# Memory attention: scores of two heads per matmul, transpositions four at a time in a two-bank tile

## The chip, the cores and the metric

The kernel runs on one core of one Trainium2 chip. The metric is the time of one execution on the device, in microseconds (us). Engines are named as in the profile: PE (TensorE, matrix products and transpositions), PEld (its loading of weights), DVE (VectorE), ACT (ScalarE), POOL (GpSimd) and SP (SyncE, which here only issues DMAs).

## The reference, cut to what matters

The reference is one decoder layer over 1024 tokens of width 1024, in float32: a mixer (spatial gating and differential attention), attention to a memory of 256 tokens, and a mixture of 32 experts. The change lies in the memory attention:

```python
q = (hq @ w_q).reshape(Bn, Sn, MEM_HEADS, MEM_HEAD_DIM) * (MEM_HEAD_DIM ** -0.5)
kv = (mem_n @ w_kv).reshape(Bn, Mn, 2, MEM_HEADS, MEM_HEAD_DIM)
k, v = kv[:, :, 0], kv[:, :, 1]
s = jnp.einsum('bqhd,bkhd->bhqk', q, k).astype(jnp.float32)
p = jax.nn.softmax(s, axis=-1)
o = jnp.einsum('bhqk,bkhd->bqhd', p.astype(v.dtype), v).reshape(Bn, Sn, MEM_WIDTH)
return o @ w_o
```

Sn is 1024 and there are 4 heads of 256 memory tokens.

## The kernel before, in words

The kernel multiplies the keys into the query weights, and the values into the output weights, ahead of time. For each head the product of w_q and the keys is a matrix of 1024 x 256 (`md`), written to DRAM by `mem_m` and read back as weights of 512 KB by the queue of SP. The scores of a tile of 128 tokens are then the normalized hidden state (`h2`, eight tiles of 128 rows) times `md`, and the probabilities of all heads times `vwd` give the result of the attention (`mem_out`). Every product of float32 is three matmuls of a rounded half and a remainder (`mm3`, lines 136 to 138); `split` makes the two halves, the rounded one by a cast on ACT (L141), the remainder by a subtraction on DVE (L142). Weights are split the same way (L280 on ACT, L281 on DVE).

The scores (`mem_scores`) go head by head. A PSUM bank of 128 x 512 holds two tiles of tokens of one head: twice 24 matmuls of 256 columns. There are 4 heads x 2 halves of 512 tokens x 2 banks, so 16 banks. After each bank DVE takes the negative maximum of each row (L971) and scales it by the row's norm (L972), ACT computes the two exponentials with their sums (L974), DVE inverts the sums (L977), and POOL multiplies the probabilities by them (L979). When a head's half is done, `mem_values` transposes the probabilities on PE: 8 transposes of 128 x 128 (L1000), the first four into one PSUM bank (`pt`), the others into a second, and each bank is split into an `om` tile (L141, L142).

[...]

The program is emitted by generators that a small planner (`Merge`) interleaves by costs and delays in its own time: a `yield 1.3, 0.0` says that work of 1.3 was emitted, and the second number holds the generator back. Which engines keep the emitted order is set by `manual_schedule`: in this stage before the change SP and POOL do, while the order of PE, DVE and ACT is set by the framework's own scheduler. A wait between engines is put in by the framework wherever a tile is written after it was read, or read after it was written.

Of the kernel before, what the change touches and what calls it, by code (L numbers as in the profile page):

```python
# [8 lines left out]
F32 = mybir.dt.float32  # L9
# [11 lines left out]
KT = 8  # L21
H = 512
# [87 lines left out]
def tile_layer(tc, a, out):  # L110
# [12 lines left out]
    def unit(name, shape, dt=F32):  # L123
        return up.tile(shape, dt, name=name, tag="u", bufs=NU)
# [4 lines left out]
    def ps1(name="ps"):  # L129
        return psum.tile([128, 512], F32, name=name, tag="ps", bufs=4)  # L130

    def ps2(name="pd"):
        return psum.tile([128, 1024], F32, name=name, tag="pd", bufs=2)

    def mm3(o, sh, sl, mh, ml, start, stop):
        mm(o, sh, mh, start=start, stop=False)  # L136
        mm(o, sh, ml, start=False, stop=False)  # L137
        mm(o, sl, mh, start=False, stop=stop)  # L138

    def split(hi, lo, src):  # L140
        nc.scalar.copy(hi, src)  # L141
        nc.vector.tensor_sub(lo, src, hi.bitcast(F32))  # L142
# [71 lines left out]
    def add_pair(w, i):  # L214
        for q in range(2):
            plan.append((w[2 * i + q], 4))

    w_in8, w_in4 = a["w_in8"], a["w_in4"]
    for item in (SEQ1 + " " + SEQ2).split():
# [15 lines left out]
        else:  # L235
            w = a["w_q_memT" if kind == "m" else "w_o_mem"]
            for k in (2 * i, 2 * i + 1):
                plan.append((w[k * 128:(k + 1) * 128, :], 1))
    for hd in range(4):
        add_pair(md, hd)  # L240
    for h in range(2):
        for f in range(8):
            add_cols(vwd, f)
# [41 lines left out]
    def take():  # L285

        j = ptr["use"]
        ptr["use"] += 1
        pump()
        k = plan[j][1]  # L290
        return [t.rearrange("p (k c) -> p k c", k=k) for t in parts.pop(j)]
# [88 lines left out]
    def mem_m(hd):  # L380

        kk = kks.pop(("m", hd))
        w = [take() for _ in range(2)]
        for g in range(2):
            mt = unit("mt", [128, 4, 256])
            for b in range(2):
                p = ps1("pp")
                for j in range(2):
                    ds_ = slice((4 * g + 2 * b + j) * 128, (4 * g + 2 * b + j + 1) * 128)
                    for d in range(2):  # L390
                        mm3(p[:, j * 256:(j + 1) * 256], w[d][0][:, 0, ds_], w[d][1][:, 0, ds_], kk[:, 0, d],
                            kk[:, 1, d], d == 0, d == 1)
                nc.scalar.copy(mt[:, 2 * b:2 * b + 2], p)
                yield 1.3, 0.0
            nc.gpsimd.dma_start(md[2 * hd + g], mt.rearrange("p k c -> p (k c)"))

    def mem_w(hd):

# [535 lines left out]
    r2c = cp.tile([128, 8], F32, name="r2c")  # L934

    def r2_cols(h):
        p = ps1()
        colsum_out(h, p)
        rsq(r2c[:, 4 * h:4 * h + 4], p[:, 0:8:2], D / 256.0, 1e-6 * 256.0, "r")
        yield 0.9, 3.0  # L940
        done.add(("r2", h))
# [2 lines left out]
    om, P, rdy = {}, {}, {}  # L944

    def mem_scores():
        for hd in range(4):
            w = [take() for _ in range(2)]
            for h in range(2):
                if 2 * hd + h - nval[0] >= 2:  # L950
                    yield 0.0, lambda: 2 * hd + h - nval[0] < 2
                pe = unit("pe", [128, 4, 256])
                mx = sm.tile([128, 16], F32, name="mx", bufs=2)
                for t2 in range(2):
                    p = ps1("pp")
                    for j in range(2):
                        t = 4 * h + 2 * t2 + j
                        ts = slice(t * 128, (t + 1) * 128)
                        for k in range(KT):
                            wh, wl = w[k // 4]  # L960
                            mm3(p[:, j * 256:(j + 1) * 256], h2[k][0][:, ts], h2[k][1][:, ts], wh[:, k % 4],
                                wl[:, k % 4], k == 0, k == KT - 1)
                            if k == 3:
                                yield 1.3, 0.0
                        if j == 0:
                            yield 1.3, 0.0
                    for x in until(("r2", h)):
                        yield x
                    p3 = p.rearrange("p (t k) -> p t k", t=2)
                    i = 2 * t2  # L970
                    red(mx[:, i:i + 2], p3, axis=AX.X, op=OP.max, negate=True)  # L971
                    tt(mx[:, i:i + 2], mx[:, i:i + 2], r2c[:, 4 * h + i:4 * h + i + 2], op=OP.mult)  # L972
                    for j in range(2):
                        nc.scalar.activation(pe[:, i + j], p3[:, j], AF.Exp, bias=mx[:, i + j:i + j + 1],  # L974
                                             scale=r2c[:, 4 * h + i + j:4 * h + i + j + 1],
                                             accum_out=mx[:, 4 + i + j:5 + i + j])
                    nc.vector.reciprocal(mx[:, 8 + i:10 + i], mx[:, 4 + i:6 + i])  # L977
                    for j in range(2):
                        nc.gpsimd.tensor_scalar(pe[:, i + j], pe[:, i + j], mx[:, 8 + i + j:9 + i + j], 0.0,  # L979
                                                op0=OP.mult, op1=OP.add)  # L980
                    if t2 == 0:
                        yield 1.3, 0.0
                P[hd, h] = pe
                rdy[hd, h] = merge.t + 6.0
                done.add(("P", hd, h))
                yield 1.3, 0.0

    nval = [0]

    def mem_values():  # L990
        for hd in range(4):
            for h in range(2):
                for x in until(("P", hd, h)):
                    yield x
                yield 0.0, max(0.0, rdy[hd, h] - merge.t)
                pe = P.pop((hd, h))
                for b in range(2):
                    p = ps1("pt")
                    for t in range(4):
                        nc.tensor.transpose(p[:, t * 128:(t + 1) * 128], pe[:, t, b * 128:(b + 1) * 128], ident)  # L1000
                    x = unit("om", [128, 2, H], F32R)
                    split(x[:, 0], x[:, 1], p)
                    om[2 * hd + b, h] = x
                    yield 0.45, 0.0
                nval[0] += 1
                if hd == 3:
                    yield 0.0, 2.0
                done.add(("om", hd, h))


    desc = cp.tile([128, 8], F32, name="desc")
# [212 lines left out]
    def mem_out(hf):  # L1224
# [67 lines left out]
        for f, k0, k1 in todo:  # L1292
            if k0 == 0:
                x2 = half("x2")
                nc.sync.dma_start(x2, x1d[f * 128:(f + 1) * 128, hs])
                if hf:
                    ahead["load"] += PF
                grp[f] = (take(), ps1("pp"), x2)
            (wh, wl), p, x2 = grp[f]
            for k in range(k0, k1):  # L1300
                if k == 6:
                    for x in until(("om", 3, hf)):
                        yield x
                if (f, k) == (7, 5):
                    for t in range(4):
                        mm(plg[:, 160 + 2 * t:162 + 2 * t], acc["x2", hf][0][:, t * 128:(t + 1) * 128], ones[:, 0:2],
                           start=False, stop=False)
                o = om[k, hf]
                mm3(p, wh[:, k], wl[:, k], o[:, 0], o[:, 1], k == 0, k == KT - 1)
                if k in (1, 3, 5):  # L1310
                    yield 1.28, 0.0
            if k1 == 8:
                fin(f, p, x2)
                yield 1.28, 0.0
# [5 lines left out]
    def mem_end(hf):  # L1320
        for x in until(("mo", hf)):
            yield x
        last, plg, store = fini[hf]
        if hf:
            man = tc.manual_schedule(engines=RM)
            man.__enter__()
        else:
            yield 0.0, 0.8
        last()
        if hf:  # L1330
            for i in range(NX):
                xg.append(unit("xg", [128, D]))
                nc.gpsimd.memset(xg[i], 0.0)
            ahead["load"] += PG
            pump()
        yield 2.0, 3.0
        for x in route(hf, plg, store):
            yield x
        if hf:
            man.__exit__(None, None, None)  # L1340
# [21 lines left out]
    def first_consts():  # L1362
# [10 lines left out]
        for x in attn_lam():  # L1373
# [14 lines left out]
    man = tc.manual_schedule(engines=ORDS[2])  # L1388
    man.__enter__()
    ahead["load"], ahead["split"] = QL, QS  # L1390
    merge.run(r2_cols(0), r2_cols(1), mem_values(), mem_scores(), mem_end(0), mem_end(1),
              seq(until(RC), now(route_consts), now(load_gfb), mem_out(0), mem_out(1)))
    man.__exit__(None, None, None)


# [379 lines left out]
```

## Time and profile before

| | |
|---|---|
| time, median of 3 runs | 1393.46 us (1392.2 to 1393.85) |
| time of the profiled execution | 1396.04 us |
| its span on the core | 1394.3 us |
| PE busy | 1322.7 us, 95% of the span |
| DVE, ACT, POOL busy | 1001.3, 836.7, 255.7 us |
| DMA | 322.39 MB, mean 231 GB/s |

The span is what the trace shows, from the first instruction to the last; the profiled execution's own time is 1.7 us longer and lies 2.6 us above the median of the runs. Busy times are sums over an engine's instructions, and those of PE are pipelined: a matmul begins before the one before it has ended, so the time that one costs on PE is read from start to start. The granted clock of PE (PEclk) is 1.00 at full speed and 0.5 at half.

### The profile page before, as it was taken

How to read it: one execution, taken by the hardware profiler on the slowest of the kernel's cores; microseconds unless marked ns; L12 is line 12 of the kernel's file. 1: busy time of each engine (PE TensorE's matmuls, PEld its weight loads, DVE VectorE, ACT ScalarE, POOL GpSimd, SP SyncE). 2: the span in 40 equal slices, each digit the busy share in tenths (PEclk: the TensorE clock that was granted, in tenths of full speed). 3: DMA queues.
4: the chain of work that ended last, by engine and by line, in shares of the span. 5: the costliest groups of instructions: out<-in, count | busy, mean ns of one | idle time of the engine just before them, and what ended most of it. 6: DMA issues, size and time to landing. Idle time of an engine off the chain costs nothing. (4 is left out here: it accounts for less than half of the span.)

```text
span 1394.3 us, 20530 instructions
## 1 busy us (share of the span) xinstructions
PE 1322.7 (95%) x7424; PEld 1146.8 (82%) x7424; DVE 1001.3 (72%) x1564; ACT 836.7 (60%) x1139; POOL 255.7 (18%) x284
## 2 busy tenths in 40 slices
PE   7999999999989999999998899999989999999981
PEld 6988998989888889998886687888778888888861
DVE  6776694767765543434365798999979999999984
ACT  6644553445455543333323587888868888888874
POOL 2521110411021321112112121111111111111110
PEclk9999999999999999999998799999999999999995
DMA  8720211320275664103799799999999699999986
GB/s 306 220 84 15 47 61 46 91 69 16 101 266 188 201 243 143 38 25 110 241 331 336 244 322 369 364 355 357 354 366 351 226 371 381 366 366 363 373 287 256
DMA packets 103226, 322.39 MB, mean 231 GB/s; under 512 B 15748, under 2 KB 23972, under 8 KB 103121
## 3 DMA queue, kind: packets, MB, share of 16 engines
q1 hardware_dynamic: 76896, 272.14, 53.4%
q0 software_dynamic: 17776, 40.51, 10.1%
q10 hardware_dynamic: 8448, 8.39, 1.8%
q8 instruction: 59, 0.97, 0.3%
q14 instruction: 47, 0.38, 0.1%
HBM read 287.10 MB, written 46.66 MB: 239 GB/s over the span
## 5 line engine op out<-in xcount | busy, mean ns | idle before, releaser
L281 DVE TENSOR_TENSOR wlo<-raw,whi 128x1024 fp32r<-128x1024 f32 (+1 forms) x469 | 559.6, 1231 | 75.3 <-ACT whi L280 62.6
L280 ACT CAST whi<-raw 128x1024 fp32r<-128x1024 f32 (+1 forms) x469 | 472.7, 1050 | 69.2 <-DVE wlo L281 11.9
L136 PE MATMUL pgu<-whi,xth 128*128 128x512 f32 x512 | 199.4, 398 | 4.3 <-ACT whi L280 3.2
L137 PE MATMUL pgu<-wlo,xth 128*128 128x512 f32 x512 | 201.2, 393 | 0.8 <-DVE wlo L281 0.8
L138 PE MATMUL pgu<-whi,xtl 128*128 128x512 f32 x512 | 201.0, 393 | 0.5 <-DVE xtl L142 0.5
L1464 POOL DMA_INDIRECT x2d<-y,idx x31 | 51.6, 1666 | 449.4 <-ACT y L1463 411.5
L136 PEld LDWEIGHTS pgu<-whi,xth 128*128 128x128 f32 x512 | 97.0, 190 | 26.0 <-ACT whi L280 5.2
L137 PEld LDWEIGHTS pgu<-wlo,xth 128*128 128x128 f32 x512 | 97.2, 190 | 22.3 <-DVE wlo L281 1.4
L138 PEld LDWEIGHTS pgu<-whi,xtl 128*128 128x128 f32 x512 | 97.0, 189 | 21.2 <-DVE xtl L142 1.2
L137 PE MATMUL py<-wlo,ht 128*128 128x512 f32 x256 | 103.7, 405 | 2.2 <-DVE wlo L281 2.2
L136 PE MATMUL py<-whi,ht 128*128 128x512 f32 x256 | 102.3, 399 | 1.5 <-ACT whi L280 0.8
L138 PE MATMUL py<-whi,ht 128*128 128x512 f32 x256 | 101.0, 394 | 0.0
L658 ACT ACTIVATE p<-p,stt 128x128 f32<-128x128 f32 (+7 forms) x64 | 49.6, 776 | 50.4 <-DVE stt L657 45.9
L136 PE MATMUL pp<-whi,hTh 128*128 128x256 f32 x256 | 74.6, 291 | 0.2 <-ACT whi L280 0.2
L137 PE MATMUL pp<-wlo,hTh 128*128 128x256 f32 x256 | 73.4, 287 | 1.3 <-DVE wlo L281 1.3
L136 PE MATMUL pp<-whi,h2h 128*128 128x256 f32 x256 | 73.1, 285 | 0.0
L138 PE MATMUL pp<-whi,hTl 128*128 128x256 f32 x256 | 73.1, 285 | 0.0
L137 PE MATMUL pp<-wlo,h2h 128*128 128x256 f32 x256 | 72.5, 283 | 0.0
L138 PE MATMUL pp<-whi,h2l 128*128 128x256 f32 x256 | 72.5, 283 | 0.0
L136 PE MATMUL pp<-hTh,whi 128*128 128x512 f32 x160 | 63.6, 397 | 0.4 <-ACT ot L710 0.4
L137 PE MATMUL pp<-hTl,whi 128*128 128x512 f32 x160 | 63.0, 394 | 0.0
L138 PE MATMUL pp<-hTh,wlo 128*128 128x512 f32 x160 | 62.8, 393 | 0.0
(365 smaller groups left out, 2942.4 us busy)
## 6 DMA issues: line engine op xcount, KB each, us to landing
raw<-in_w_gate SPq DMA_DIRECT2D x128, 512.0 KB
raw<-in_w_up SPq DMA_DIRECT2D x128, 512.0 KB
raw<-in_w_down SPq DMA_DIRECT2D x128, 512.0 KB
raw<-in_w_in SPq DMA_DIRECT2D x19, 512.0 KB
raw<-in_w_kv_mem SPq DMA_DIRECT2D x16, 512.0 KB
raw<-vwd SPq DMA_DIRECT2D x16, 512.0 KB
raw<-in_w_q_memT SPq DMA_DIRECT2D x8, 512.0 KB
raw<-in_w_out SPq DMA_DIRECT2D x8, 512.0 KB
```

What stands on the lines that cost most here:

```text
L136: mm(o, sh, mh, start=start, stop=False)
L137: mm(o, sh, ml, start=False, stop=False)
L138: mm(o, sl, mh, start=False, stop=stop)
L280: nc.scalar.copy(hi[:, c], raw[:, c])
L281: ahead.get("lo", nc.vector).tensor_tensor(lo[:, c], raw[:, c], hi[:, c].bitcast(F32), op=OP.subtract)
L658: nc.scalar.activation(pe[:, :nk], pe[:, :nk], AF.Exp, bias=stt[:, 2 + m:3 + m], scale=slopes[hd], accum_out=stt[:, 4 + m:5 + m])
L1464: nc.gpsimd.indirect_dma_start(out=x2d[:, :], out_offset=bass.IndirectOffsetOnAxis(ap=idx[:, e:e + 1], axis=0), in_=y, in_offset=None, bou ...
```

## The change

- `mem_scores` works on two heads at a time: a bank holds one tile of tokens of both heads, from 24 matmuls of 512 columns. There are still 16 banks, but 384 matmuls instead of 768. Four weight tiles are taken per pair of heads, where two were taken per head.
- `md` is laid out by pairs of heads; `mem_m` therefore writes each 512 KB product by two DMAs with pieces of 1 KB instead of one.
- The multiplication of the probabilities by the inverted sums moves from POOL to DVE (32 TENSOR_SCALARs of 128 x 256).
- `mem_values` takes a two-bank tile per head and half; four transposes go to its first bank, four to the second, and by the planner's numbers (`yield 0.45, 1.3`) six matmuls of the scores stand between the two sets.
- Up to the end of the scores PE keeps the emitted order (`mem_order`); `mem_out` waits for `om` of the third and the fourth head apart.

```diff
-    for hd in range(4):
-        add_pair(md, hd)
+    for q in range(8):
+        plan.append((md[q], 2))
...
-            nc.gpsimd.dma_start(md[2 * hd + g], mt.rearrange("p k c -> p (k c)"))
+            for q in range(2):
+                nc.gpsimd.dma_start(
+                    md[4 * (hd // 2) + 2 * g + q].rearrange("p (k h t) -> p k h t", k=2, h=2)[:, :, hd % 2],
+                    mt[:, 2 * q:2 * q + 2])
...
     def mem_scores():
-        for hd in range(4):
-            w = [take() for _ in range(2)]
+        for hp in range(2):
+            w = [take() for _ in range(4)]
             for h in range(2):
...
+                for t in range(4):
                     p = ps1("pp")
+                    ts = slice((4 * h + t) * 128, (4 * h + t + 1) * 128)
+                    for k in range(KT):
+                        wh, wl = w[k // 2]
+                        mm3(p, h2[k][0][:, ts], h2[k][1][:, ts], wh[:, k % 2], wl[:, k % 2], k == 0, k == KT - 1)
+                        if k in (1, 3, 5):
+                            yield 1.36, 0.0
...
-                        nc.gpsimd.tensor_scalar(pe[:, i + j], pe[:, i + j], mx[:, 8 + i + j:9 + i + j], 0.0,
-                                                op0=OP.mult, op1=OP.add)
+                        nc.vector.tensor_scalar(pe[j][:, t], pe[j][:, t], mx[:, 2, 2 * t + j:2 * t + j + 1], None,
+                                                op0=OP.mult)
...
     def mem_values():
...
-                for b in range(2):
-                    p = ps1("pt")
+            pd = ps2("pt")
+            for b in range(2):
+                p = pd[:, b * H:(b + 1) * H]
...
-                    yield 0.45, 0.0
+                yield 0.45, 1.3
...
+    mem_order = tc.manual_schedule(engines={ET.PE})
+    mem_order.__enter__()
...
-              seq(until(RC), now(route_consts), now(load_gfb), mem_out(0), mem_out(1)))
+              seq(until(RC), now(mem_order.__exit__, None, None, None), now(route_consts), now(load_gfb), mem_out(0), mem_out(1)))
```

How the instructions stand on PE around the first transposes, before the change. A row is the place in PE's order, the line, the operation, its output and inputs (`pt` the transposed probabilities, `pe` the probabilities, `pp` a bank of scores), and the engines whose semaphores it waits for:

```order
3175 L137 MATMUL pp_5542<-wlo_5301,h2h_5304 128x256
3176 L138 MATMUL pp_5542<-whi_5300,h2l_5305 128x256
3177 L1000 MATMUL pt_5598<-ident_71,pe_5426 128x128 [waits Pool_49] x4
3178 L1000 MATMUL pt_5606<-ident_71,pe_5426 128x128 [waits DVE_49,Activation_49]
3179 L1000 MATMUL pt_5606<-ident_71,pe_5426 128x128 x3
3180 L136 MATMUL pp_5614<-whi_5227,h2h_4433 128x256 [waits DVE_49,Activation_49]
3181 L137 MATMUL pp_5614<-wlo_5228,h2h_4433 128x256
3182 L138 MATMUL pp_5614<-whi_5227,h2l_4434 128x256
3183 L136 MATMUL pp_5614<-whi_5227,h2h_4582 128x256
```

The eight transposes of the first head's first half stand in a row, into two tiles (`pt_5598`, `pt_5606`), and the next bank of scores follows. After the change, the same place:

```order
3152 L138 MATMUL pp_5582<-whi_5390,h2l_5313 128x512
3153 L1004 MATMUL pt_5614<-ident_71,pe_5406 128x128 [waits DVE_49] x4
3154 L136 MATMUL pp_5622<-whi_5235,h2h_4437 128x512 [waits PE_49,Activation_49]
3155 L137 MATMUL pp_5622<-wlo_5236,h2h_4437 128x512
3156 L138 MATMUL pp_5622<-whi_5235,h2l_4438 128x512
3157 L136 MATMUL pp_5622<-whi_5235,h2h_4588 128x512
3158 L137 MATMUL pp_5622<-wlo_5236,h2h_4588 128x512
3159 L138 MATMUL pp_5622<-whi_5235,h2l_4589 128x512
3160 L1004 MATMUL pt_5614<-ident_71,pe_5406 128x128 [waits DVE_49]
3161 L1004 MATMUL pt_5614<-ident_71,pe_5406 128x128 x3
3162 L136 MATMUL pp_5622<-whi_5308,h2h_4740 128x512
```

The first four transposes stand alone, then six matmuls of the next bank, then the second four into the same tile, `pt_5614`, with a wait for DVE at the first of them. The lines are those of the changed kernel (L1004 there is L1000 before).

The order of DVE around the same place before the change (`mx` holds the maxima and sums, `om` the split of the transposes):

```order
739 L971 TENSOR_REDUCE mx_5541<-pp_5542 128x2 [waits PE_49]
740 L972 TENSOR_TENSOR mx_5541<-mx_5541,r2c_91 128x2 [waits DVE_49]
741 L977 RECIPROCAL mx_5541<-mx_5541 128x2 [waits Activation_49]
742 L142 TENSOR_TENSOR om_5603<-pt_5598,om_5603 128x512 [waits Activation_49]
743 L142 TENSOR_TENSOR om_5611<-pt_5606,om_5611 128x512 [waits Activation_49]
744 L281 TENSOR_TENSOR wlo_5673<-raw_5420,whi_5672 128x1024 [waits DMAHW2_49,Activation_49]
```

After the bank's maximum, scaling and inversion come the subtractions of the transposes (`om`). After the change, where L973, L974, L979 and L981 are the maximum, its scaling, the inversion and the scaling of the probabilities:

```order
755 L973 TENSOR_REDUCE mx_5581<-pp_5582 128x2 [waits PE_49]
756 L974 TENSOR_SCALAR mx_5581<-mx_5581,r2c_91 128x2 [waits DVE_49]
757 L979 RECIPROCAL mx_5581<-mx_5581 128x2 [waits Activation_49]
758 L981 TENSOR_SCALAR pe_5579<-pe_5579,mx_5581 128x256 [waits DVE_49]
759 L981 TENSOR_SCALAR pe_5580<-pe_5580,mx_5581 128x256
760 L142 TENSOR_TENSOR om_5619<-pt_5614,om_5619 128x512 [waits Activation_49]
761 L142 TENSOR_TENSOR om_5633<-pt_5614,om_5633 128x512 [waits Activation_49]
762 L142 TENSOR_TENSOR om_5647<-pt_5642,om_5647 128x512 [waits Activation_49]
```

The subtraction that empties the first half of `pt_5614` (`om_5619`) stands behind all DVE work of the bank of scores that has just ended, the two new TENSOR_SCALARs included; it is that subtraction which the second four transposes wait for.

## Rows read from the trace of the kernel before

**Rows 1.** Windows: us, then busy of PE, PEld, DVE, ACT, POOL, clock, DMA share, GB/s
```profile
540.00:560.00 20.00, 20.00 (x170) 20.00 (x170) 7.95 (x32) 3.84 (x10) 1.88 (x4) 1.00 0.19 70
700.00:750.00 50.00, 50.00 (x279) 42.34 (x277) 27.55 (x69) 15.55 (x23) 11.98 (x12) 1.00 0.92 326
750.00:777.00 27.00, 16.16 (x109) 14.98 (x109) 17.81 (x63) 6.00 (x10) 6.73 (x6) 0.59 0.83 281
```

**Rows 2.** Groups by line and form, 538 to 660 us: names, shapes, count | busy us, mean ns
```profile
L136 PE MATMUL pp<-whi,h2h 128*128 128x256 f32 x256 | 73.1, 285 | 0.0
...
L979 POOL TENSOR_SCALAR pe<-pe,mx 128x256 f32<-128x256 f32 x32 | 15.1, 484 | 88.5 <-DVE mx L977 88.5
```

**Rows 3.** Timeline of PE at a bank's end: start us, busy us, line, names
```profile
555.07 0.28 PE L136 MATMUL pp<-whi,h2h 128*128 128x256 f32 x1
...
558.55 0.28 PE L138 MATMUL pp<-whi,h2l 128*128 128x256 f32 x1
558.67 1.04 PE L1000 MATMUL pt<-ident,pe 128*128 128x128 f32 x8
559.46 0.36 PE L136 MATMUL pp<-whi,h2h 128*128 128x256 f32 x1
```

**Rows 4.** Timeline of PE in the projection ahead, 512 columns a matmul
```profile
535.79 0.39 PE L136 MATMUL pp<-mixh,whi 128*128 128x512 f32 x1
...
537.15 0.39 PE L136 MATMUL pp<-mixh,whi 128*128 128x512 f32 x1
```

**Rows 5.** Timeline of VectorE after that bank, 558 to 563 us
```profile
558.87 0.69 DVE L971 TENSOR_REDUCE mx<-pp 128x2 f32<-128x512 f32 x1 [3.38 <-PE pp L138]
559.60 0.16 DVE L972 TENSOR_TENSOR mx<-mx,r2c 128x2 f32<-128x2 f32 x1
561.09 0.17 DVE L977 RECIPROCAL mx<-mx 128x2 f32<-128x2 f32 x1 [1.33 <-ACT pe L974]
561.56 1.29 DVE L142 TENSOR_TENSOR om<-pt,om 128x512 fp32r<-128x512 f32 x2 [0.31 <-ACT om L141]
```

**Rows 6.** Timeline of ScalarE after that bank
```profile
559.85 0.57 ACT L974 ACTIVATE pe<-pp,mx,r2c 128x256 f32<-128x256 f32 x1 [4.56 <-DVE mx L972]
...
560.86 0.20 ACT L974 ACTIVATION_READ_ACCUMULATOR pe<-pp,mx,r2c 128x1 f32 x1
560.95 1.07 ACT L141 CAST om<-pt 128x512 fp32r<-128x512 f32 x2
```

**Rows 7.** Groups by form of VectorE, whole span: its TENSOR_SCALARs nearest in form
```profile
L837 DVE TENSOR_SCALAR v<-v,mv,rs 128x128 f32<-128x128 f32 x32 | 8.6, 342 | 0.1
...
L1053 DVE TENSOR_SCALAR ra<-ra,c_norm_ffn 128x36 f32<-128x36 f32 x8 | 1.3, 236 | 0.0
```

**Rows 8.** Windows around three idle stretches of PE in the expert stage
```profile
789.00:792.00 3.00, 1.51 (x10) 0.83 (x7) 1.90 (x3) 2.46 (x4) 0.99 (x1) 1.00 0.85 288
792.00:796.00 4.00, 3.87 (x10) 3.08 (x11) 2.44 (x3) 1.76 (x2) 0.00 (x0) 0.57 0.74 229
842.00:845.00 3.00, 1.40 (x6) 0.58 (x5) 1.30 (x2) 2.37 (x3) 0.00 (x0) 1.00 1.03 418
845.00:848.00 3.00, 3.00 (x15) 2.52 (x16) 3.00 (x4) 3.00 (x4) 0.00 (x0) 1.00 1.00 384
1020.00:1024.00 4.00, 1.19 (x5) 0.41 (x3) 1.21 (x1) 2.29 (x3) 0.00 (x0) 1.00 1.02 403
1024.00:1028.00 4.00, 3.93 (x10) 3.11 (x11) 3.58 (x4) 3.32 (x4) 0.00 (x0) 0.57 0.94 363
```

**Rows 9.** Windows of the expert stage, its start and its middle
```profile
770.00:780.00 10.00, 8.37 (x34) 7.54 (x35) 6.58 (x9) 2.75 (x4) 5.00 (x4) 0.56 0.54 151
1100.00:1200.00 100.00, 100.00 (x479) 83.33 (x478) 92.01 (x86) 81.52 (x91) 17.73 (x12) 1.00 1.01 373
```

**Rows 10.** DMA issues, the products of the keys: queue, count, KB, us to landing
```profile
md<-mt POOLq DMA_DIRECT2D x8, 512.0 KB, 6.3
```

**Rows 11.** Timeline of VectorE at the start of the scores
```profile
538.64 2.35 DVE L281 TENSOR_TENSOR wlo<-raw,whi 128x1024 fp32r<-128x1024 f32 x2
```

More of the change, by code (lines that the diff above doesn't have):

```diff
@@ L936, in r2_cols @@
     def r2_cols(h):
+        yield 0.0, (1.3, 5.0)[h]
         p = ps1()
@@ L946, in mem_scores @@
     def mem_scores():
-        for hd in range(4):
-            w = [take() for _ in range(2)]
+        for hp in range(2):
+            w = [take() for _ in range(4)]
             for h in range(2):
[L950 to L954, printed above, removed]
-                    p = ps1("pp")
[L956 to L966, printed above, removed]
+                if 4 * hp + 2 * h - nval[0] >= 3:
+                    yield 0.0, lambda: 4 * hp + 2 * h - nval[0] < 3
+                pe = [unit("pe", [128, 4, 256]) for _ in range(2)]
+                mx = sm.tile([128, 3, 8], F32, name="mx", bufs=2)
+                for t in range(4):
+                    p = ps1("pp")
+                    ts = slice((4 * h + t) * 128, (4 * h + t + 1) * 128)
[4 more added lines that the diff above has]
+                            yield 1.36, 0.0
@@ L967, in mem_scores @@
                     for x in until(("r2", h)):
                         yield x
[L969 to L972, printed above, removed]
+                    p3 = p.rearrange("p (j k) -> p j k", j=2)
+                    i = slice(2 * t, 2 * t + 2)
+                    r = r2c[:, 4 * h + t:4 * h + t + 1]
@@ L973, in mem_scores @@
+                    red(mx[:, 0, i], p3, axis=AX.X, op=OP.max, negate=True)
+                    nc.vector.tensor_scalar(mx[:, 0, i], mx[:, 0, i], r, None, op0=OP.mult)
                     for j in range(2):
[L974 to L977, printed above, removed]
+                        c = slice(2 * t + j, 2 * t + j + 1)
+                        nc.scalar.activation(pe[j][:, t], p3[:, j], AF.Exp, bias=mx[:, 0, c], scale=r,
+                                             accum_out=mx[:, 1, c])
@@ L978, in mem_scores @@
+                    nc.vector.reciprocal(mx[:, 2, i], mx[:, 1, i])
                     for j in range(2):
-                        nc.gpsimd.tensor_scalar(pe[:, i + j], pe[:, i + j], mx[:, 8 + i + j:9 + i + j], 0.0,
-                                                op0=OP.mult, op1=OP.add)
[L981 to L986, printed above, removed]
+                        nc.vector.tensor_scalar(pe[j][:, t], pe[j][:, t], mx[:, 2, 2 * t + j:2 * t + j + 1], None,
+                                                op0=OP.mult)
@@ L988, in tile_layer @@
+                    if t < 3:
+                        yield 1.36, 0.0
+                for j in range(2):
+                    P[2 * hp + j, h] = pe[j]
+                    rdy[2 * hp + j, h] = merge.t + 6.0
+                    done.add(("P", 2 * hp + j, h))
+                yield 1.36, 0.0
     nval = [0]
     def mem_values():
[L991 to L996, printed above, removed]
-                for b in range(2):
-                    p = ps1("pt")
[L999 to L1003, printed above, removed]
-                    yield 0.45, 0.0
[L1005 to L1008, printed above, removed]
+        for hd, h in [(2 * hp + j, h) for hp in range(2) for h in range(2) for j in range(2)]:
+            for x in until(("P", hd, h)):
+                yield x
+            yield 0.0, max(0.0, rdy[hd, h] - merge.t)
+            pe = P.pop((hd, h))
+            pd = ps2("pt")
+            for b in range(2):
+                p = pd[:, b * H:(b + 1) * H]
+                for t in range(4):
+                    nc.tensor.transpose(p[:, t * 128:(t + 1) * 128], pe[:, t, b * 128:(b + 1) * 128], ident)
+                x = unit("om", [128, 2, H], F32R)
+                split(x[:, 0], x[:, 1], p)
+                om[2 * hd + b, h] = x
+                yield 0.45, 1.3
+            nval[0] += 1
+            if hd > 1:
+                yield 0.0, 2.0
+            done.add(("om", hd, h))
@@ L1300, in mem_out @@
             for k in range(k0, k1):
-                if k == 6:
-                    for x in until(("om", 3, hf)):
+                if k in (4, 6):
+                    for x in until(("om", k // 2, hf)):
                         yield x
```

## The prediction

> **What bounds the kernel now.** I read the windows first. In the memory attention PE is busy all the time at the full clock, while DVE and ACT work 7.95 and 3.84 of 20 us; it stays so through the attention's output, 700 to 750 us [rows 1]. So what counts in this stage is PE's stream: time saved on PE is saved, and any wait that PE is given shows in full. Then comes a stretch at clock 0.59 in which PE works 16.16 of 27 us [rows 1]; there the routing runs as a chain behind the last token, so a shift of PE's end is handed on. Behind it the experts run with PE at 100 of 100 us and the DMA queues full [rows 9].
>
> Next I read what one matmul costs. The groups by form give 285 ns for each of three lines with 256 matmuls, the 768 of the scores [rows 2]. That is a duration in a pipeline, not a price. From start to start, 30 matmuls of 256 columns begin between 555.07 and 558.55, 3.48 us over 29 steps, 0.120 us each [rows 3]; 512 columns begin 1.36 us apart over 6 steps, 0.2267 us [rows 4].
>
> Last I read the chain that follows a bank, on DVE and ACT, since the new order hangs something on it. Take T as the start of the transposes, 558.67 [rows 3]. The maximum starts at T+0.20, its scaling at T+0.93, the exponentials at T+1.18, the second sum is read at T+2.39, the inversion runs from T+2.42 to T+2.59 [rows 5, 6].
>
> **The change part by part.** *The matmuls.* 768 x 0.120 = 92.2 us go, 384 x 0.2267 = 87.1 us come: -5.1 us, all of it on PE's path.
>
> *The transposes.* There are still 64. Eight of them, with the change into and out of them, take 0.79 us from 558.67 to 559.46, near 0.10 each [rows 3]. They now come in 16 sets, not 8. The trace shows no set of four; a further change of form can cost nothing or the 0.08 us by which the first matmul behind the eight starts later than the pitch of those before would have it. I take 8 x 0.08 = +0.6 us, with 0 as the other end.
>
> *The new wait.* The second four transposes of a head write into the tile that the first four wrote, and stand six matmuls behind them. Their first waits for DVE, and DVE's order puts the subtraction that empties the first half behind all work of the bank that has just ended: maximum, scaling, inversion and two TENSOR_SCALARs. PE is through with four transposes and six matmuls at T + 0.40 + 6 x 0.2267 = T+1.8. DVE is at the inversion's end at T+2.59. Then come the two TENSOR_SCALARs of 128 x 256, which DVE has not done before in this form. Below, the nearest row is 236 ns for 128 x 36; beside it, 342 ns for 128 x 128 with two column operands [rows 7]; above, POOL's 484 ns for this very work [rows 2]. I take 0.35, the row nearest in form, and keep 0.236 and 0.484 as ends. Two of them with small gaps end at T+3.33, the subtraction (1.29 us for two [rows 5], 0.69 for one with its tail) at T+4.06, and PE goes on at T+4.1. The cast on ACT, which it also needs, is ready before, since ACT is free at T+2.39 and takes some 0.55 [rows 6]. So PE stands for 4.1 - 1.8 = 2.3 us, 2.07 to 2.57 by the ends for the TENSOR_SCALAR. Queued behind the waiting transposes on PE is everything: the rest of the bank, so its maximum, and so on; nothing passes them.
>
> The fourth set of a pair waits for the subtraction of the third. DVE has to do the second half's subtraction first (its cast begins when the second set ends, 0.5 us, then 0.65), then the third's; I get T+7.6 to T+7.9 against PE's T+7.7: 0 to 0.2 us, taken as 0.2. For the third head's first half the fourth set's subtraction stands ahead of the inversion, and I count nothing.
>
> How often: a group of four sets comes behind the first bank that follows each half of a pair, that is for pair 0 half 0, pair 0 half 1 and pair 1 half 0, each behind a bank's end as above. The last half's transposes fall into the output stage, where DVE has no bank to finish, and matmuls of `mem_out` stand between; I count nothing there. Sum: 3 x 2.3 + 2 x 0.2 = +7.3 us, 6.2 to 8.1 by the ends (3 x 2.07, and 3 x 2.57 + 0.4).
>
> *The clock.* PE stood 1.5 of 3 us at 789 to 792 and 2.8 of 4 us at 1020 to 1024, and each time the next window of 4 us shows clock 0.57; 1.6 of 3 us at 842 to 845 left it at 1.00 [rows 8]. [...] A stall of 2.3 us in one piece stands between the idle times of the two that lost the clock. I give each of the three stalls three chances in four: likeliest is two, +3.4 us, the ends are 0 and +5.1.
>
> *What I cost at nothing.* The TENSOR_SCALARs as load: DVE is busy 7.95 of 20 us [rows 1]; 32 x 0.35 is 11 us over 100 and only their place in the chain counts. POOL loses 15.1 us of work [rows 2], and nobody on the path waited for it as a load. The eight additional DMAs of `md` on POOL's queue, and their smaller pieces: one lands in 6.3 us [rows 10], and the load that reads it on SP's queue is issued only behind the projections and the output products that follow; if that cover were gone it would be a few us once. The start: the first bank needs four weight tiles, so the split of the later two, 2.35 us from 538.64 [rows 11], is needed within the first bank instead of the second. They are done at 541.0, and PE, which still works off small matmuls there, by my estimate reaches them about 1 us later; without the cover, 1 to 2 us. The loads of `md` are as many, as large and in the same place of SP's queue.
>
> **Sum.** -5.1 + 0.6 + 7.3 + 3.4 = +6.2 us against the profiled execution's 1396.04 us, 1402.2. That execution lies 2.6 us above the median of the runs, and I carry the difference over to the median: 1393.46 + 6.2 = 1399.7 us. Ends of the unknown costs: -5.1 + 0 + 6.2 + 0 = +1.1 and -5.1 + 0.6 + 8.1 + 5.1 = +8.7, so 1394.6 to 1402.2 for this case alone. What a measurement of this kernel can tell from no change is about 0.2%, 2.8 us.
>
> [...] DVE reads the first bank of a two-bank tile while PE would write the second. The order shows a wait there all the same, and in the trace no PE write into a half-read tile of this kind can be seen to stand. [...]
>
> [...]
>
> **The rivals.** *No stall: the halves don't hold each other up.* If the wait that the order shows is met by older work of DVE, or DVE comes to the subtraction by T+1.8, PE runs through: -5.1 + 0.6 = -4.5 us, 1389.0. For it: the halves are different banks, and nothing but the tile's name joins them. Against: DVE's order has the subtraction behind an inversion that cannot begin before the second sum at T+2.39 [rows 6]. It decides as soon as the subtraction ends before T+1.8. Chance 0.16, some of it for what I have missed on the cheap side.
>
> *Stalls, but made good behind.* PE may lose 1 to 7 us and the experts start on weights that were loaded in the meantime. For it: the DMA share in the middle of the experts is 1.01, so a DMA bound could swallow a later start [rows 9]. Against: at 770 to 780 the share is 0.54 with PE just starting [rows 9], so the loads had already run ahead and stood waiting for free buffers. Or no stall costs the clock and the stalls are the shorter ones. Then the time is within 2.8 us, about 1393.5 to 1395. Chance 0.23.
>
> *The clock falls at each of the three stalls, and the TENSOR_SCALAR is POOL's 0.484:* +8.7, 1402.2. It is an end of the forecast's own case, chance 0.12 of it.
>
> *The durations are the price.* 384 x 0.39 against 768 x 0.285 is -69 us, 1324. Starts speak against it: PE's rows begin every 0.120 us, not every 0.285. Chance 0.01.
>
> **How the numbers follow.** My forecast, stalls that the end of the kernel sees, 0.60 in all; no stall 0.16, made good 0.23, durations 0.01. Faster by over 0.2%: 0.16 + 0.01 = 0.17. Same: 0.23. Slower: 0.60. The range reaches from 1390.5, between the first rival and the second, to the forecast's upper end, 1402.2, rounded up to 1402.5; it leaves out the first rival and little above. The likeliest case's own range is 1394.6 to 1402.2.
>
> **What would show it.** In the changed kernel's trace the scores' matmuls should start 0.227 us apart; three times PE should be idle some 2.3 us right before a set of transposes, released by DVE's subtraction, and the window after it should show a clock below 1.00 about twice. The two TENSOR_SCALARs should be 0.24 to 0.48 us. The scores should end some 6 us later than now, and the experts start later by as much. I am wrong if PE has no idle time in the scores, if the releaser there is another, or if the lead or lag at the scores' end is not found again at the first expert.

## The result, and the profile after

| | before | after |
|---|---|---|
| time, median of 3 runs | 1393.46 us (1392.2 to 1393.85) | 1405.2 us (1403.75 to 1406.28) |
| profiled execution, its span | 1396.04, 1394.3 us | 1406.28, 1404.6 us |

The changed kernel is slower: the ratio is 1.0079, with a 95% interval of 1.0063 to 1.0095; the medians lie 11.7 us apart. The forecast had the sign, +6.2 us, and a range that ended at 1402.5.

The answer to [rows 1, 3, 4] first. After the change PE in the scores (start, busy us, operation, tiles; in brackets the idle time before and who ended it):

```profile
567.58 0.60 PE L1004 MATMUL pt<-ident,pe 128*128 128x128 f32 x4
567.93 0.48 PE L136 MATMUL pp<-whi,h2h 128*128 128x512 f32 x1
568.25 0.40 PE L137 MATMUL pp<-wlo,h2h 128*128 128x512 f32 x1
...
568.95 0.39 PE L137 MATMUL pp<-wlo,h2h 128*128 128x512 f32 x1
569.18 0.40 PE L138 MATMUL pp<-whi,h2l 128*128 128x512 f32 x1
571.54 0.66 PE L1004 MATMUL pt<-ident,pe 128*128 128x128 f32 x4 [1.96 <-DVE om L142]
```

The matmuls of 512 columns start 0.23 us apart, as priced. The second four transposes come 1.96 us late, released by DVE's subtraction. There are three such stalls and no fourth: 1.96, 1.98 and 2.04 us. The same place on DVE, to set beside [rows 5]:

```profile
567.78 0.69 DVE L973 TENSOR_REDUCE mx<-pp 128x2 f32<-128x512 f32 x1 [2.35 <-PE pp L138]
568.50 0.23 DVE L974 TENSOR_SCALAR mx<-mx,r2c 128x2 f32<-128x2 f32 x1
570.06 0.17 DVE L979 RECIPROCAL mx<-mx 128x2 f32<-128x2 f32 x1 [1.33 <-ACT pe L977]
570.26 0.61 DVE L981 TENSOR_SCALAR pe<-pe,mx 128x256 f32<-128x256 f32 x2
570.80 0.68 DVE L142 TENSOR_TENSOR om<-pt,om 128x512 fp32r<-128x512 f32 x1
```

And on ACT, to set beside [rows 6]:

```profile
568.83 0.56 ACT L977 ACTIVATE pe<-pp,mx,r2c 128x256 f32<-128x256 f32 x1 [4.24 <-DVE mx L974]
...
569.83 0.20 ACT L977 ACTIVATION_READ_ACCUMULATOR pe<-pp,mx,r2c 128x1 f32 x1
569.93 0.58 ACT L141 CAST om<-pt 128x512 fp32r<-128x512 f32 x1
```

The chain is the one that was worked out: maximum, scaling, two exponentials, inversion, two TENSOR_SCALARs, then the subtraction, which ends at 571.48. The cast on ACT starts only at 569.93, behind the exponentials, and ends at 570.51; so the two TENSOR_SCALARs (0.61 us for both) hold the subtraction up for only some 0.3 us more than the cast does.

The third stall cost the clock, the first two did not (length, busy us of PE, PEld, DVE, ACT, POOL, granted clock, DMA share, GB/s):

```profile
594.00:598.00 4.00, 2.02 (x13) 1.40 (x11) 2.13 (x6) 1.68 (x5) 0.00 (x0) 1.00 0.00 0
620.00:624.00 4.00, 1.96 (x12) 1.35 (x10) 2.19 (x6) 1.68 (x5) 0.00 (x0) 1.00 0.00 0
624.00:628.00 4.00, 4.00 (x14) 3.21 (x13) 0.69 (x1) 0.59 (x1) 3.15 (x5) 0.57 0.22 30
628.00:632.00 4.00, 4.00 (x22) 3.10 (x21) 1.61 (x3) 1.43 (x4) 0.00 (x0) 1.00 0.14 14
```

PE did about the same at 594 and at 620, and only at 620 was it followed by the lower level: 0.57 over 4 us, which is 3.4 us at half the clock (0.50 in each half us from 624.5 to 627.5).

Now the ends of the stages. These are three single matmuls on PE after the change, the last of the projection ahead, of the attention's output and of the experts:

```profile
536.45 0.39 PE L138 MATMUL pp<-mixh,wlo 128*128 128x512 f32 x1
...
752.71 0.39 PE L138 MATMUL pp<-om,wlo 128*128 128x512 f32 x1
...
1364.85 0.39 PE L138 MATMUL py<-whi,ht 128*128 128x512 f32 x1
```

Before, the same three start at 537.61, 749.49 and 1365.62. From the first to the second it is 211.9 us before and 216.3 after, so the stage has become 4.4 us longer. From the second to the third, the stretch of the routing and the experts, it is 616.1 us before and 612.1 after, 4.0 shorter; 2.7 of these 4.0 us are idle time of PE in the experts, 12.3 us before and 9.6 after. So the third starts even a little earlier than before. Behind it come 28.7 us before and 39.7 after, and these 11.0 us are more than the 10 by which the spans differ. POOL at the end, before:

```profile
1320.81 1.71 POOL L1464 DMA_INDIRECT x2d<-y,idx  x1 [15.76 <-ACT y L1463]
1338.99 2.49 POOL L1464 DMA_INDIRECT x2d<-y,idx  x1 [16.48 <-ACT y L1463]
1350.42 2.41 POOL L1464 DMA_INDIRECT x2d<-y,idx  x1 [8.93 <-ACT whi L280]
1358.49 1.07 POOL L1528 DMA_INDIRECT xg<-x2d,idx  x1 [5.67 <-PE pt L1444]
```

And after:

```profile
1322.24 1.63 POOL L1471 DMA_INDIRECT x2d<-y,idx  x1 [15.79 <-ACT y L1470]
1340.50 16.16 POOL L1471 DMA_INDIRECT x2d<-y,idx  x1 [16.62 <-ACT y L1470]
1361.79 1.56 POOL L1471 DMA_INDIRECT x2d<-y,idx  x1 [5.13 <-DMA x2d<-y,idx]
1368.58 1.06 POOL L1535 DMA_INDIRECT xg<-x2d,idx  x1 [5.22 <-issue]
```

These are the issues of indirect DMAs: each expert's result is added to the output rows in DRAM by a scatter that POOL issues. Expert 29's takes POOL 16.16 us instead of 2.49. Expert 30's waits for it, and the loads of the finished rows wait for both: SP issues the first of them at 1367.94 instead of 1357.85. DVE during that time, before:

```profile
1337.09 0.68 DVE L142 TENSOR_TENSOR ht<-pt,ht 128x512 fp32r<-128x512 f32 x1
1337.69 9.16 DVE L281 TENSOR_TENSOR wlo<-raw,whi 128x1024 fp32r<-128x1024 f32 x8
1347.12 1.23 DVE L281 TENSOR_TENSOR wlo<-raw,whi 128x1024 fp32r<-128x1024 f32 x1 [0.26 <-ACT whi L280]
1350.16 6.29 DVE L281 TENSOR_TENSOR wlo<-raw,whi 128x1024 fp32r<-128x1024 f32 x5 [1.81 <-ACT whi L280]
```

And after:

```profile
1338.65 0.68 DVE L142 TENSOR_TENSOR ht<-pt,ht 128x512 fp32r<-128x512 f32 x1
1339.25 15.98 DVE L281 TENSOR_TENSOR wlo<-raw,whi 128x1024 fp32r<-128x1024 f32 x14
1355.68 0.75 DVE L1444 SCALAR_TENSOR_TENSOR hh<-pgu,tab,hh 128x512 f32<-128x512 f32 x1 [0.46 <-PE pgu L138]
1357.80 0.69 DVE L142 TENSOR_TENSOR ht<-pt,ht 128x512 fp32r<-128x512 f32 x1 [1.36 <-ACT ht L141]
```

After the change DVE does 14 weight splits without a gap, 1339.25 to 1355.22, and POOL's issue, begun at 1340.50 beside the second of them, ends at 1356.66, 1.44 us after the last. Before, the run was 8 splits long, and POOL got through within it: its issue began beside the second split there too, and ended 1.44 us after that split's end at 1340.05. The code of both is the same there.

### The profile page after: what moved, and what is told of

Its sections match the earlier page's. It is cut to its first block, busy times and chain, and to the rows that moved or that the text cites. A ratio compares the mean times of both kernels' runs of the same rounds, so it can differ in the third digit from the quotient of the medians.

```text
span 1404.6 us, 19772 instructions
## 1 busy us (share of the span) xinstructions
PE 1319.8 (94%) x7040; PEld 1126.2 (80%) x7040; DVE 1010.1 (72%) x1596; ACT 837.5 (60%) x1139; POOL 260.0 (19%) x260
## 5 line engine op out<-in xcount | busy, mean ns | idle before, releaser
L1471 POOL DMA_INDIRECT x2d<-y,idx x31 | 64.3, 2075 | 445.4 <-ACT y L1470 411.3
L882 POOL TENSOR_TENSOR acc<-acc,sq 128x512 f32<-128x512 f32 x24 | 32.5, 1353 | 156.0 <-ACT sq L878 156.0
L137 PEld LDWEIGHTS py<-wlo,ht 128*128 128x128 f32 x256 | 48.6, 190 | 12.4 <-DVE wlo L281 4.1
L136 PEld LDWEIGHTS py<-whi,ht 128*128 128x128 f32 x256 | 48.6, 190 | 11.4 <-ACT ht L141 0.9
```

What stands on the lines that cost most here:

```text
L882: nc.gpsimd.tensor_tensor(acc[key][0], acc[key][0], sq, op=OP.add)
L1471: nc.gpsimd.indirect_dma_start(out=x2d[:, :], out_offset=bass.IndirectOffsetOnAxis(ap=idx[:, e:e + 1], axis=0), in_=y, in_offset=None, bou ...
```

## The experiments

Two theories. A: most of the loss is the scatter that is held up beside DVE's unbroken run; the scores themselves cost about what was forecast. B: the loss is the stalls in the scores, handed on to the end. All ratios are against the kernel before on the same chip.

**A hole in DVE's run.** In the changed kernel, behind the scatter of expert 29:

```diff
+        if e == NE - 3:
+            nc.gpsimd.memset(flag, 0.0)
+            nc.vector.tensor_copy(flag2, flag)
```

> The changed kernel, and in the last experts VectorE waits once (a copy of 128x1 whose input GpSimd writes behind its scatter-add of expert 29), so that VectorE's run of weight splits has a hole while that scatter is issued. Theory A (most of the loss is GpSimd's scatter being held up beside VectorE's unbroken run): the scatter's issue falls from 16.2 us to 3 at most and the time to 1394 to 1398 us. Theory B (the loss is the three stalls in the scores, handed on to the end): the time stays at 1404 to 1407 us, since nothing in the scores is changed.

Measured: 1398.14 us, ratio 1.0034 (1.0021 to 1.0047), at the upper end of theory A's range. POOL:

```profile
1340.56 2.36 POOL L1471 DMA_INDIRECT x2d<-y,idx  x1 [15.28 <-ACT y L1470]
1342.34 0.70 POOL L1475 MEMSET flag<- 128x1 f32 x1
1350.94 1.70 POOL L1471 DMA_INDIRECT x2d<-y,idx  x1 [7.91 <-DMA x2d<-y,idx]
1359.89 1.06 POOL L1540 DMA_INDIRECT xg<-x2d,idx  x1 [7.26 <-PE pt L1451]
```

The scatter takes 2.36 us, and 7 of the 11.7 us are gone, with the scores untouched. Theory B is out as the whole cause. (The scatter also began at another place against the splits, 0.29 us after the start of one, 0.12 without the hole.) In the scores this execution even lost more of the clock, at each of the three stalls:

```profile
540.00:640.00 100.00, 94.01 (x423) 76.78 (x422) 42.42 (x120) 29.71 (x75) 3.68 (x6) 0.95 0.09 27
```

The granted clock is 0.95 over these 100 us (10 us at half, three times the 3.4); in the changed kernel's first profile it was 0.98:

```profile
540.00:640.00 100.00, 94.00 (x435) 76.48 (x435) 45.11 (x125) 31.45 (x79) 3.69 (x6) 0.98 0.12 36
```

> The kernel before with the same hole in VectorE's run. Theory A: the scatter took only 2.5 us there, so the hole wins nothing and costs up to 1.5 us: 1392 to 1396 us. Theory B says the same, as nothing was held up before.

The same edit in the kernel before: 1391.94 us, 0.9992 (0.9982 to 1.0002). Nothing is to be had there, as both theories had it.

**The stalls away: 18 matmuls between the sets.**

```diff
-                yield 0.45, 1.3
+                yield 0.45, 4.0
```

> The changed kernel with 18 matmuls of the scores between the two sets of transposes of a head instead of 6 (the planner's delay 4.0 instead of 1.3). Both theories: PE's three stalls of 2.0 us go, and the half clock with them, so the scores end 6 to 8 us earlier. Theory B: the whole of it is found again at the end, 1397 to 1400 us. Theory A: the end depends on how VectorE's run and the scatter meet there; either near 1388 to 1393 us, or held up again, 1400 to 1405.

Measured: 1386.3 us, 0.9954 (0.9938 to 0.9971). PE does not wait in the scores any more:

```profile
540.00:640.00 100.00, 100.00 (x474) 82.69 (x473) 47.92 (x130) 32.65 (x83) 3.67 (x6) 1.00 0.17 58
```

The stage is 207.6 us long against 211.9 before: -4.3 us is what the change of the matmuls and transposes is worth without the stalls (forecast -4.5). The scatter took 2.48 us. So one number in the planner is worth 19 us: stalls, clock, and the held-up scatter. The time is below what either theory gave, and the stage's 4.3 us are not all of the 6.9 us gained; the experts' stretch is short here too, 610.6 us.

> Both edits together. Theory A: without stalls and without the held-up scatter, 1386 to 1392 us, below the kernel before. Theory B: like the run with 18 matmuls alone, 1397 to 1400 us.

Both: 1385.14 us, 0.9940 (0.9923 to 0.9956). This is the fastest version, 8 us below the kernel before and a little below the expected range. Between this run and the first one, both with the hole, lie only the stalls and the clock: 13.0 us. So the loss has two parts. Without stalls and hold-up the change is worth -8.1 us; the stalls add 13.0, the held-up scatter some 7 more.

**Memsets between the splits: no wait, but a broken run.** With the tile `flag` as above:

```diff
             parts[j] = (hi, lo)
+            if len(plan) - 16 <= j < len(plan) - 8:
+                nc.vector.memset(flag, 0.0)
```

> The changed kernel with a memset of 128x1 on VectorE behind each of eight weight splits of the last two experts: no wait, but VectorE's run is broken by instructions that read no SBUF. Theory A (GpSimd's scatter can't write while VectorE goes from one two-input subtraction straight into the next): the scatter's issue falls from 16.2 us to 3 us at most, the time to 1396 to 1399 us, as with the hole. A rival, A2 (it was the wait that helped, by ordering VectorE behind GpSimd, or by shifting the last experts): the scatter stays at 10 us or more, 1403 to 1407 us.

Measured: 1401.17 us, 1.0043 (1.0022 to 1.0065); the ten runs lie between 1396.1 and 1403.0, the profiled one is the lowest. In it:

```profile
1338.08 2.56 POOL L1474 DMA_INDIRECT x2d<-y,idx  x1 [16.71 <-ACT y L1473]
1348.96 2.24 POOL L1474 DMA_INDIRECT x2d<-y,idx  x1 [8.32 <-ACT whi L281]
```

2.56 us. The weights came as in the changed kernel (the next product on ACT, y, waited for PE, 0.38 us, as it does there), and the memsets wait for nothing; so in this execution it was not the waiting that helped. Theory A's reason, that the scatter can't write beside splits that follow each other, no profile shows: what is seen is how long the issue took, and in the kernel before it got through inside a run of 8 splits without a gap. The median was a little above the forecast. The other runs were not profiled, and whether the scatter was held up in the slower of them is not known.

> The changed kernel once more, nothing changed. If the held-up scatter belongs to this kernel's timing, the runs lie again at 1403 to 1407 us and the scatter takes over 10 us in the profile; if it was a chance of single executions, part of the runs lie near 1397 us.

The changed kernel again, on the same chip: 1407.17 us, 1.0088 (1.0063 to 1.0113), no run below 1402.07.

```profile
1338.74 16.13 POOL L1471 DMA_INDIRECT x2d<-y,idx  x1 [16.69 <-ACT y L1470]
1360.46 1.56 POOL L1471 DMA_INDIRECT x2d<-y,idx  x1 [5.58 <-DMA x2d<-y,idx]
```

The held-up scatter belongs to this kernel: 16.13 us again. Against the memsets, on the same chip, the medians lie 6 us apart.

**A tile of its own for each set.**

```diff
-            pd = ps2("pt")
             for b in range(2):
-                p = pd[:, b * H:(b + 1) * H]
+                p = ps2("pt")[:, :H]
```

> The changed kernel with a tile of its own for each set of four transposes (the same two buffers of two banks in turn), six matmuls between the sets as before. If the stall comes from the two halves sharing a tile, the three stalls of 2.0 us go and the third set of the first two groups waits some 0.5 us for the first set's subtraction: PE idle in the scores 1.0 instead of 6.0 us, no half clock there, and the scores end 6 to 7 us earlier. If VectorE's lateness as such is the cause, some 4 us of idle stay. At the end: 1386 to 1390 us if the scatter gets through, some 10 more if not.

Measured: 1389.45 us, 0.9971 (0.9950 to 0.9992). With the same six matmuls between the sets PE's idle time in the scores falls from 6.0 to 0.3 us, and the first subtraction stands behind the same work on DVE as in the changed kernel:

```profile
540.00:640.00 100.00, 99.69 (x470) 81.97 (x470) 48.66 (x133) 33.85 (x85) 3.79 (x6) 1.00 0.19 60
```

So it is the shared tile that makes the stall. The wait forecast for the third set, 0.5 us twice, came with 0.14 and 0.17.

> 18 matmuls between the sets and the memsets between the splits. Theory A: no stall, no held-up scatter, as with the hole or a little better, 1384 to 1387 us.

Measured: 1387.53 us, 0.9954 (0.9936 to 0.9972), one us above the forecast's end. The scatter took 2.51 us.

**The scaling back on POOL, with the hole.**

> The changed kernel with the scaling of the probabilities on GpSimd, as before, and the hole in VectorE's run in the last experts. If the two TENSOR_SCALARs (2 x 0.35 us) lie in the chain that the second four transposes wait for, the stalls shrink from 2.0 us; the cast on ScalarE then ends last, so to 1.5 to 1.7 us rather than by the full 0.7: 1 us in all, 1396 to 1398 us. If they lie beside it, the stalls stay at 2.0.

Measured: 1394.86 us, 1.0023 (1.0012 to 1.0033), below the range; the stalls are 1.72, 1.80 and 1.86 us. They shrink by 0.2 us each, not by the 0.7 that the two TENSOR_SCALARs last: the cast on ACT ends nearly as late. The rest of the 3 us against the first hole goes, by the two profiles, to the clock, lost at one stall here and at three there.

**Does the phase of POOL against DVE decide?** In the held-up profiles the scatter began 0.12 and 0.15 us behind the start of a subtraction, in before 0.165. Six runs of the kernel before shift that by memsets on DVE: behind the first split of the last run (two, four, then one), behind the three splits around it, or behind two or three splits ahead of the run. The first of them:

```diff
+            if j == len(plan) - 15:
+                for _ in range(2):
+                    nc.vector.memset(flag, 0.0)
```

> The kernel before with two memsets of 128x1 on VectorE, behind the first weight split of the last run, so that the next subtraction starts some 0.03 to 0.1 us later against GpSimd's scatter; nothing else. In the runs so far the scatter got through where it began 0.16 us or more after the start of a subtraction (before, and four others) and was held up where it began 0.12 to 0.15 us after it in an unbroken run. Theory A (a race of the two engines at that point, settled by their phase): the scatter is held up for 14 to 17 us and the kernel takes 1400 to 1405 us, for 0.1 us of work. Rival (the held-up scatter comes with the changed memory attention, for instance by where the loads stand): nothing happens, 1392 to 1395 us.

> The same with four memsets, a shift of 0.06 to 0.2 us. Theory A: held up as with two, unless the shift takes the scatter's start ahead of the subtraction's, and then it gets through: 1400 to 1405 or 1392 to 1395 us, with the phase in the trace on the side that goes with it. Rival: 1392 to 1395 us.

Both shifted too far: the scatter began 0.06 and 0.31 us ahead of the subtraction and took 1.56 us; 1392.54 and 1393.45 us, no difference (0.9998 and 1.0003). This told nothing of the phase in question.

> The kernel before with one memset of 128x1 on VectorE behind the first split of the last run. Where single memsets stood between the splits they lengthened the step from one subtraction to the next by some 0.015 us, so the scatter should begin some 0.15 us behind the start of a subtraction, where it was held up in the changed kernel (0.12 and 0.15), instead of 0.165. Theory A (the phase of the two engines decides): held up for 14 to 17 us, 1400 to 1405 us. Rival (the hold-up belongs to the changed memory attention): 1392 to 1395 us.

> The same with one memset behind each of the three splits ahead: a shift of some 0.045 us, the scatter some 0.12 us behind a subtraction's start, as in the changed kernel's first profile. Theory A: held up, 1400 to 1405 us. Rival: 1392 to 1395 us.

They hit it, 0.156 and 0.128 us, and the scatter got through in 2.50 and 2.53 us: 1394.72 (1.0013) and 1393.7 us (1.0008). But a memset stood beside the scatter's start in both.

> The kernel before with single memsets on VectorE behind three splits ahead of the last run and none in it, so that nothing stands between the two subtractions beside which the scatter begins: a shift of some 0.03 to 0.045 us, the scatter 0.12 to 0.14 us behind the start, and the subtraction before it at -1.25 to -1.27, as in the changed kernel's two profiles. If the phase decides (in the run with three memsets one stood right at that place, and may have let the scatter in), it is held up: 1400 to 1405 us. If not, 1392 to 1395 us, and the phase is out as the cause.

> The same with two memsets ahead: a shift of 0.03 us, 0.13 to 0.14 us behind. As there: 1400 to 1405 us if the phase decides, 1392 to 1395 us if not.

Here the memsets stand ahead of the run and the run is clean: 0.143 and 0.149 us, through in 2.51 us; 1393.31 (0.9995) and 1392.45 us (0.9993):

```profile
1339.31 2.51 POOL L1467 DMA_INDIRECT x2d<-y,idx  x1 [16.48 <-ACT y L1466]
```

The scatter began within 0.005 us of where it was held up in the repeat of the changed kernel. The phase alone is not the cause.

> The changed kernel with two memsets in a row behind the first split of the last run, as in the run on the kernel before that shifted the subtractions by 0.2 us; the run itself stays unbroken behind them. Theory A: the scatter now begins ahead of its subtraction, gets through in 1.6 to 2.5 us, and the kernel takes 1396 to 1400 us. Rival (the length of the run decides, or the loads): still held up, 1403 to 1408 us.

In the changed kernel the two memsets moved the scatter ahead of the subtraction; it took 1.56 us, and the kernel 1399.9 us, 1.0048 (1.0030 to 1.0067). That fits theory A. POOL and DVE in that profile:

```profile
1342.11 1.56 POOL L1475 DMA_INDIRECT x2d<-y,idx  x1 [16.14 <-ACT y L1474]
...
1340.85 1.22 DVE L282 TENSOR_TENSOR wlo<-raw,whi 128x1024 fp32r<-128x1024 f32 x1
1342.01 0.20 DVE L286 MEMSET flag<- 128x1 f32 x2
1342.20 8.04 DVE L282 TENSOR_TENSOR wlo<-raw,whi 128x1024 fp32r<-128x1024 f32 x7
1351.61 1.23 DVE L282 TENSOR_TENSOR wlo<-raw,whi 128x1024 fp32r<-128x1024 f32 x1 [1.37 <-ACT whi L281]
```

The long run has gone with the hold-up: after seven splits DVE waits 1.37 us for ACT, and that for its weights. So the 14 in a row may be an effect as well as a cause. The likely reading, which was not tried by itself: while the scatter is not issued, its traffic does not stand in the way of the last weights; they come early, DVE never comes to a stop, and POOL is kept out. The traces fit it: from 1341 to 1356 us after the change no packet moves on POOL's DMA queue, while before, from 1340 to 1355, there are 191.

> 18 matmuls between the sets of transposes, and the two memsets: no stall in the scores and the scatter ahead of its subtraction. 1384 to 1387 us, the level of the fastest so far.

1385.74 us, 0.9953 (0.9936 to 0.9969), as expected.

## Why the prediction was wrong, point by point

**What bounds the stage** was right: PE's stream, and each wait shows in full.

**The matmuls and transposes**, -5.1 + 0.6: right as a sum. Without the stalls the stage is 4.3 us shorter (4.0 in two other versions without them), and the rival that took the durations for the price, -69 us, is out.

**The wait** was right in its place, its releaser and its number, and a little too long: 3 x 2.0 = 6.0 us instead of 7.3. PE came to it at T+1.99 instead of T+1.8, and DVE's subtraction began at T+3.22 instead of T+3.37, since the TENSOR_SCALARs overlap (351 ns each in the groups by form, but 0.61 us for the pair). The fourth sets did not wait at all. That the cast on ACT is ready before held, but by 0.3 us only; so most of the TENSOR_SCALARs' time lies beside it, which the run with the scaling on POOL shows too.

**The two halves of a tile**: the kernel waits until the first half is emptied, 1.96 us, before it writes the second, because the wait is put in by tile. With two tiles it is gone: PE is idle for 0.3 us in the scores. What the chip would do without any guard was not tried.

**The clock**: two of three was called likeliest, though three chances in four for each stall make three falls as likely as two (0.42 each). It was one of three in the profile and three of three in the execution with the hole; over all six profiles with such stalls, 10 of 18. Stalls of one length went both ways. No run shows the 1.7 us for each fall, of which the +3.4 and the +5.1 are made, as time lost. The granted clock would give it, again 0.57 over 4 us, so (1 - 0.57) x 4 = 1.7; but the stage with three falls is only 2.5 us longer than that with one (218.8 and 216.3 us; 3.1 in another execution with three), so 1.2 to 1.5 for each.

**The sum in the stage**: with one fall, at the 1.7 of the granted clock, and the measured terms, -4.3 + 6.0 + 1.7 = +3.4 us; the stage was 4.4 longer. Half of the 1 us left is that the idle time is counted from a matmul's modelled end: the next would have started at 569.41, PE stands from 569.57. The other half is not assigned.

**The step that failed** is the end of the sum. With the sentence "a shift of PE's end is handed on" everything behind the stage was taken to come later by the shift and to stay as it was otherwise, and so nothing behind it got a term. The runs show two things there. From the experts' last matmul to the end it is 39.7 and 40.0 us in the two profiles of the changed kernel, 28.7 before: 11 us, for a scatter held up for 16 instead of 2.5 us. And the stretch of the routing and the experts is 4.0 us shorter. Between the first two profiles the stage's +4.4 becomes +4.4 - 4.0 + 11.0, and 1.2 us were gained ahead of it: the 10 us between the spans. By the medians the missing term is 7 us, and the range was drawn without it.

That a shift is handed on holds by itself. The first expert's first matmul starts at 780.5 us instead of 776.8, so the stage's loss is still there. With the hole in both, the version with stalls and the one without are 11.2 us apart in the stage (218.8 and 207.6) and 13.2 at the end (spans of 1395.8 and 1382.6). So the rival that had the shift "made good behind" did not happen either: the stretch of the experts is short with stalls (611.7 to 614.2 us in six profiles, 612.6 on average) and without (610.6 to 616.0 in five, 612.9), against 612.8 to 619.3 in the eight profiles of the kernel before and its versions, 616.3 on average. Why the changed kernel is faster there is not found.

With the scatter out of the way the changed kernel is 4.9 us slower than before (2.9 to 6.5), where the sum had 6.2. That they lie so near is luck in part: in that profile the stage lost 6.9 us, with the clock gone three times, and the experts gave 3.4 back.

**What stays open** is why the scatter is held up in this kernel. Shown: it is so in both profiles of the changed kernel; in the profiles with a hole, with memsets between the splits or with an earlier start of the scatter it is not, and each of these edits also moved the scatter's start against the splits. Not shown: what brings it on. The kernel before is not caught at the same phase, and the versions without stalls are not caught at all. Once it is held up, the long run keeps it so: both times the issue ends 1.44 us after the last split of the run. Why it does not get in at the end of the split beside which it begins, 1.1 us after its start, is not found. Ahead of it the two held-up profiles differ from before in that ACT waits for PE before it writes y (0.37 and 0.40 us), so the scatter comes later against the weights; but the run with the memsets between the splits had that too.

## What to carry to other kernels

Two sets of instructions that share one tile wait for each other even where they touch different banks (here 1.96 to 2.04 us, three times); put the second set behind the time at which the first is emptied, read from the chain on the engine that empties it, or give it a tile of its own. A matmul's price is its start-to-start time (0.2267 us for 512 columns, where the row's duration is 0.39), which here foretold the gain of matmuls and transposes to 0.2 to 0.5 us. And a change that shifts a kernel by a few us can wake something far behind it: look in the rows for instructions whose time already varies (2.49 and 2.41 us for the last two scatters before the change, 1.93 and 1.71 for the two ahead of them, 1.58 or 1.59 for most of the others), and give such a tail a term or a wider range.

## What the runs showed of the hardware

The issue of a scatter on POOL took 1.56 us where DVE stood idle (1361.79 after the change). Where it began beside a running split and got through, it ended 1.44 us after the end of that split, whether another split followed or a hole: with 1.05 us of the split left it took 2.49 us in the kernel before, with 0.93 left 2.36 in the run with the hole, with 1.08 left 2.51 in the run with three memsets ahead. Where it began 0.05 to 0.31 us ahead of a split, in four profiles with memsets, it took 1.56 us again, and the splits beside it kept their 1.22 to 1.23 us. In the two held-up executions 1.10 and 1.07 us of the split were left, and the issue was passed over at the ends of twelve splits: it ended 1.44 us after the last split of the run, at 1355.22 and 1353.44. DVE in the second of them:

```profile
1337.46 15.97 DVE L281 TENSOR_TENSOR wlo<-raw,whi 128x1024 fp32r<-128x1024 f32 x14
```

Why the issue waits for a split that is running and not for one that begins after it, and why it was passed over at those twelve ends, is not shown.
